# A two-layer float32 encoder on one core: the MLP's first product moved to seven block products, its hidden units taken in blocks of 3 and 4 pairs of chunks, sums into the residual stream by adding DMAs

## The chip, the cores and the metric

The kernel runs on one core of a Trainium2 chip. The metric is the device time of one execution in microseconds (us); the median of three runs is given below. The profile is of one more execution of the same program. Its engines are called PE (TensorE, with PEld for the loading of weights into it), DVE (VectorE), ACT (ScalarE), POOL (GpSimd) and SP (SyncE, which here only issues DMAs).

## What is computed

The input is x, 512 tokens of 1024 features in float32. Two layers follow, each made of a mixing part (differential attention and a recurrent branch side by side), a cross-attention over 256 memory tokens, and an MLP. The change concerns the end of each layer:

```
x = x + ox @ xa_wo                       # 1024 -> 1024, end of the cross-attention
hm = rms_norm(x, g_mlp)
x = x + square(relu(hm @ mlp_w1)) @ mlp_w2     # 1024 -> 4096 -> 1024
```

After the second layer comes a final RMS norm.

## The kernel before, in words

**Layout.** The residual stream lies feature-major in eight tiles `x[0]` to `x[7]` of 128 features by 512 tokens ("chunks"). A float32 product is made of three matmuls of rounded parts: each operand is split into a high part (ACT copies it with rounding) and a low part (DVE subtracts the high part), and PE adds high x high, high x low and low x high into one PSUM bank (`split`, line 429; `gemm_fm`, line 472).

**Two kinds of product.** `gemm_fm` makes one output chunk of 128 features by 512 tokens: 8 input chunks x 3 matmuls of 512 columns. Its weights need one load of 512 KB (`raw_weight`, line 439), one ACT copy and one DVE subtraction of 1024 elements per partition. `seven` (line 992) makes two output chunks at once as a 2 x 2 block product in seven block products instead of eight: inputs are taken in pairs of chunks, the tokens in two halves of 256 (`LO`, `HI`), and each of the seven products is (number of pairs) x 3 matmuls of 256 columns, 84 in all with four pairs. The sums of blocks that this needs are made on both sides: `right_pair` (line 957) makes for the weights three splits of 1024 elements, one of 512 and four sums of 512; `left_pair` (line 937) makes for one pair of input chunks three splits of 512 elements, one of 256 and four sums of 256, and leaves seven tiles. The results are seven half-tile DVE additions from PSUM into `x`.

**The stage around the change** (lines 1334 to 1360). Four `seven` add `ox @ xa_wo` to `x`; each chunk of `x` is then scaled and split by `prep_x` (line 559), which also adds its square to the norm's sum. Then the MLP's 4096 hidden units are taken in four blocks of eight chunks. `mlp_pair` (line 1185) makes two hidden chunks by two `gemm_fm` from the 16 tiles of split `x`, one DVE instruction each for ReLU and the norm's factor `rb`, one ACT square each, and then `left_pair`. For each block four `seven` add its part of the second product into `x`.

**Buffers.** Tag `b`, 62 tiles of 128 x 512 (line 37), holds nearly everything above: split `x`, hidden pairs and temporaries. Weights have 3 raw tiles, 3 high, 3 low and 4 tiles `pt` for sums; PSUM has 3 banks `mm` and 5 banks `at`.

**What sets the order.** The functions don't issue instructions; they record them with their dependences. `ISSUE` (lines 54 on) is a permutation, written out by hand for all recorded operations, and `Plan.order` and `Plan.emit` (lines 371 and 380) issue in that order. So every instruction of the kernel has line 391 in the profile, and its rows are told apart by tiles. Each engine works through its part of this order strictly; buffers come free as their last reader ends. Lines 522 to 525 issue eight small matmuls (`WARM`) on a constant tile at the start, whose result nobody reads. Ten weight tiles are loaded with POOL's queue, whose second load subtracts through a DMA that adds (`weight_dma`, line 449).

## Time and profile before

| what | value |
|---|---|
| median of 3 runs | 1442.62 us (1441.48 to 1444.51) |
| the profiled execution, its own time | 1441.38 us |
| its span in the profile | 1439.6 us |
| PE busy | 1419.9 us, 99% |
| PEld busy | 1238.2 us, 86% |
| DVE busy | 1157.9 us, 80% |
| ACT busy | 771.4 us, 54% |
| POOL busy | 44.1 us, 3% |
| mean DMA rate | 110 GB/s |

A row of grouped instructions reads: line, engine, operation, tile written <- tiles read, shape, count | busy us, mean ns of one | idle us of the engine before them and what ended it. A row of the timeline reads: start in us, length in us, engine, line, operation, tiles, shape, count, and in brackets the idle time before it with its releaser. A row of windows reads: stretch, its length, then busy us and (count) for PE, PEld, DVE, ACT and POOL, the granted share of PE's clock, the DMA engines' mean busy share and GB/s.

### The profile page before, as it was taken

How to read it: one execution, taken by the hardware profiler on the slowest of the kernel's cores; microseconds unless marked ns; L12 is line 12 of the kernel's file. 1: busy time of each engine (PE TensorE's matmuls, PEld its weight loads, DVE VectorE, ACT ScalarE, POOL GpSimd, SP SyncE). 2: the span in 40 equal slices, each digit the busy share in tenths (PEclk: the TensorE clock that was granted, in tenths of full speed). 3: DMA queues.
4: the chain of work that ended last, by engine and by line, in shares of the span. 5: the costliest groups of instructions: out<-in, count | busy, mean ns of one | idle time of the engine just before them, and what ended most of it. 6: DMA issues, size and time to landing. Idle time of an engine off the chain costs nothing.

```text
span 1439.6 us, 21603 instructions
## 1 busy us (share of the span) xinstructions
PE 1419.9 (99%) x8358; PEld 1238.2 (86%) x8358; DVE 1157.9 (80%) x2027; ACT 771.4 (54%) x1201; POOL 44.1 (3%) x69
## 2 busy tenths in 40 slices
PE   9999999999999999999999999999999999999997
PEld 7887887889989899898988879888898898989986
DVE  6899994669879596888868999755796886959797
ACT  5598864346454343435536987543554534435343
POOL 1000110000000000000000010000000000000001
PEclk9999999999999999999999999999999999999998
DMA  6455643211332323232334565432023223232322
GB/s 204 120 147 143 180 139 96 93 54 60 103 116 75 118 88 119 87 113 94 117 86 150 139 163 173 126 103 70 33 89 117 88 103 117 74 124 82 118 74 88
DMA packets 50262, 157.73 MB, mean 110 GB/s; under 512 B 6384, under 2 KB 8560, under 8 KB 50160
## 3 DMA queue, kind: packets, MB, share of 16 engines
q1 hardware_dynamic: 47136, 145.61, 30.8%
q0 software_dynamic: 2880, 10.49, 3.3%
q8 instruction: 66, 1.08, 0.3%
q14 instruction: 36, 0.29, 0.1%
q10 hardware_dynamic: 144, 0.26, 0.0%
HBM read 141.65 MB, written 2.10 MB: 100 GB/s over the span
## 4 chain that ended last, share of the span: by engine, by line
PE 81%; DVE 5%; DMA 1%; issue 1%; ACT 1%; POOL 0%; DVEq 0%; ACTq 0%; POOLq 0%
PE mm L391 61%; PE at L391 20%; DVE b L391 4%; DMA wlo<-in_W 1%; DVE s L391 1%; DVE wlo L391 1%; DVE pt L391 1%; ACT b L391 0%; DMA wraw<-in_W 0%; POOL s L391 0%; ACT whi L391 0%; ACT pt L391 0%; ACT wlo L391 0%; DVE c_x L391 0%; ACT rb L391 0%
## 5 line engine op out<-in xcount | busy, mean ns | idle before, releaser
L391 PE MATMUL mm<-b,whi 128*128 128x512 f32 (+1 forms) x3640 | 944.4, 348 | 1.3 <-ACT b L391 1.0
L391 PEld LDWEIGHTS mm<-b,whi 128*128 128x128 f32 x3640 | 622.1, 188 | 92.2 <-ACT b L391 1.4
L391 PE MATMUL mm<-b,wlo 128*128 128x512 f32 (+1 forms) x1820 | 629.6, 346 | 0.0
L391 PEld LDWEIGHTS mm<-b,wlo 128*128 128x128 f32 x1820 | 341.6, 188 | 47.8
L391 ACT ACTIVATE whi<-wraw 128x1024 fp32r<-128x1024 f32 (+1 forms) x205 | 213.6, 1044 | 234.1 <-PE mm L391 142.0
L391 DVE TENSOR_TENSOR wlo<-wraw,whi 128x1024 fp32r<-128x1024 f32 (+1 forms) x205 | 246.1, 1205 | 54.1 <-ACT whi L391 53.4
L391 DVE TENSOR_TENSOR b<-b,b 128x512 fp32r<-128x512 f32 (+3 forms) x420 | 241.2, 590 | 18.1 <-ACT b L391 14.3
L391 ACT ACTIVATE b<-b 128x512 fp32r<-128x512 f32 (+2 forms) x312 | 178.5, 596 | 123.4 <-DVE b L391 120.2
L391 ACT ACTIVATE whi<-pt 128x1024 fp32r<-128x1024 f32 x80 | 84.6, 1060 | 120.0 <-DVE pt L391 64.1
L391 PE MATMUL at<-b,whi 128*128 128x256 f32 x648 | 120.9, 279 | 0.0
L391 DVE TENSOR_TENSOR c_x<-c_x,mm 128x256 f32<-128x256 f32 (+1 forms) x176 | 76.2, 441 | 45.0 <-PE mm L391 44.2
L391 DVE TENSOR_TENSOR wlo<-pt,whi 128x1024 fp32r<-128x1024 f32 x80 | 97.5, 1220 | 6.0 <-ACT whi L391 5.1
L391 PEld LDWEIGHTS at<-b,whi 128*128 128x128 f32 x648 | 100.4, 189 | 2.1
L391 DVE SCALAR_TENSOR_TENSOR b<-mm,rb 128x512 f32<-128x512 f32 x80 | 54.8, 688 | 58.9 <-PE mm L391 53.2
L391 PE MATMUL at<-b,wlo 128*128 128x256 f32 x324 | 90.3, 279 | 0.0
L391 ACT ACTIVATE b<-at,s 128x512 f32<-128x512 f32 (+2 forms) x100 | 61.1, 616 | 38.1 <-DVE s L391 29.5
L391 PE MATMUL at<-b,pt 128*128 128x256 f32 x480 | 73.2, 279 | 0.0
L391 PEld LDWEIGHTS at<-b,pt 128*128 128x128 f32 x480 | 64.5, 188 | 1.6
L391 PE MATMUL at<-b,b 128*128 128x256 f32 (+1 forms) x320 | 64.2, 328 | 0.8 <-DVE pt L391 0.5
L391 DVE TENSOR_REDUCE s<-at 128x1 f32<-128x512 f32 (+1 forms) x80 | 54.1, 683 | 11.0 <-PE at L391 10.9
L391 PEld LDWEIGHTS at<-b,wlo 128*128 128x128 f32 x324 | 60.9, 188 | 0.0
L391 DVE TENSOR_TENSOR pt<-pt,wraw 128x512 f32<-128x512 f32 x80 | 54.9, 686 | 0.3
(129 smaller groups left out, 1275.6 us busy)
## 6 DMA issues: line engine op xcount, KB each, us to landing
wraw<-in_W SPq DMA_DIRECT2D x239, 512.0 KB, 3.3
b<-b SPq DMA_DIRECT2D x96, 128.0 KB, 3.9
whi<-in_W POOLq DMA_DIRECT2D x10, 512.0 KB, 4.7
wlo<-in_W POOLq DMA_DIRECT2D x10, 512.0 KB, 5.3
wraw<-in_memT SPq DMA_DIRECT2D x4, 512.0 KB, 4.4
out_T<-b SPq DMA_DIRECT2D x16, 128.0 KB, 1.8
c_x<-in_xT SPq DMA_DIRECT2D x7, 256.0 KB, 5.3
wraw<-in_W SPq DMA_DIRECT2D x6, 256.0 KB, 4.7
```

The source lines that it names most:

```text
L391: getattr(self.engines[op.eng], m)(*a, **k)
```

## The change

The first product of the MLP is made by the seven products too: `mlp_pair` takes the split `x` as four pairs (`left`, 4 x 7 tiles), uses `right_pair` on two weight tiles, and combines the seven results of 256 tokens into two hidden chunks. It returns them before `left_pair`, which is now made at the head of each block. The hidden units come in five blocks of 3, 3, 3, 3 and 4 pairs, so `right_pair` and `seven` work on widths of 768 for the first four, and `mlp_w2` is laid out to match. The additions into `x` become, for three of the four `seven` after the cross-attention and for all but the last `seven` of the MLP in each layer, an ACT copy of the PSUM half (negated where it is subtracted) and a DMA of POOL's queue that adds it to `x` in SBUF. The eight starting matmuls go. `ISSUE` is written anew as a whole (its string is not printed).

```diff
--- before.py
+++ after.py
@@ -32,8 +32,9 @@
 T_XO = 52
 T_W1 = 60
 T_W2 = 92
-T_G = 124
-NT = 126
+BLOCKS = (3, 3, 3, 3, 4)
+T_G = T_W2 + 8 * len(BLOCKS)
+NT = T_G + 2
 NRAW = 3
 NB = 62
 NW = 3
@@ -46,138 +47,167 @@
 LAG = 2
 POOL_OUT = (0, 1)
 DMA_T = (1, 4, 13, 36, 51)
-WARM = 8
+XO_FAR = (0, 2, 4)
+FAR = (4, 6)
 
...
@@ -436,14 +466,14 @@
 
     pre = {}
 
-    def raw_weight(l, t, ahead=None):
+    def raw_weight(l, t, ahead=None, w=1024):
         raw = plan.tile("wraw", [P, 1024], F32)
         if ahead:
             for h in range(2):
                 cs = slice(h * 512, h * 512 + 512)
                 SP.dma_start(out=raw[:, cs], in_=W[l * NT + t][:, cs])
         else:
-            SP.dma_start(out=raw, in_=W[l * NT + t])
+            SP.dma_start(out=raw[:, :w], in_=W[l * NT + t][:, :w])
         return raw
 
     def weight_dma(l, t):
@@ -517,12 +547,6 @@
     G.memset(ones, 1.0)
     mhalf = C([P, 4], F32, "mhalf")
     G.memset(mhalf, -0.5)
-
-
-    warm = AT()
-    with plan.group():
-        for _ in range(WARM):
-            PE.matmul(warm[:, :P], ones, ones, start=True, stop=True)
 
     class Norm:
 
@@ -954,59 +978,76 @@
                 5: (sh[:, LO], sl[:, LO]), 6: (sh[:, HI], sl[:, HI]),
                 7: (uh[:, LO], ul[:, LO]), 3: (uh[:, HI], ul[:, HI])}
 
-    def right_pair(l, ta, tb):
-
-        ra, rb_ = raw_weight(l, ta), raw_weight(l, tb)
-        b11, b21 = (ra.split_free(4, 2, P)[:, :, i, :] for i in range(2))
-        b12, b22 = (rb_.split_free(4, 2, P)[:, :, i, :] for i in range(2))
-
-        def hl():
-            return plan.tile("whi", [P, 1024], F32R), plan.tile("wlo", [P, 1024], F32R)
-
-        ah, al = hl()
-        split(ah, al, ra)
+    def right_pair(l, ta, tb, n=4):
+
+
+        w, m = n * 2 * P, n * P
+        ra, rb_ = raw_weight(l, ta, w=w), raw_weight(l, tb, w=w)
+        b11, b21 = (ra[:, :w].split_free(n, 2, P)[:, :, i, :] for i in range(2))
+        b12, b22 = (rb_[:, :w].split_free(n, 2, P)[:, :, i, :] for i in range(2))
+
+        def split_w(src):
+            hi, lo = plan.tile("whi", [P, 1024], F32R), plan.tile("wlo", [P, 1024], F32R)
+            split(hi[:, :w], lo[:, :w], src[:, :w])
+            return hi, lo
+
+        def halves(t):
+            v = t[:, :w].split_free(2, n, P)
+            return v[:, 0], v[:, 1]
+
+        ah, al = split_w(ra)
         t12 = plan.tile("pt", [P, 1024], F32)
-        t1, t2 = (t12.split_free(2, 4, P)[:, i] for i in range(2))
+        t1, t2 = halves(t12)
         V.tensor_tensor(t1, b11, b12, op=ALU.add)
         V.tensor_tensor(t2, t1, b22, op=ALU.add)
-        th, tl = hl()
-        split(th, tl, t12)
+        th, tl = split_w(t12)
         t34 = plan.tile("pt", [P, 1024], F32)
-        t3, t4 = (t34.split_free(2, 4, P)[:, i] for i in range(2))
+        t3, t4 = halves(t34)
         V.tensor_tensor(t3, b12, b22, op=ALU.add)
         V.tensor_tensor(t4, t2, b21, op=ALU.add)
         dh = plan.tile("pt", [P, 1024], F32R)
-        dv = dh.split_free(2, 4, P)
-        split(dv[:, 0], dv[:, 1], b22)
-        uh, ul = hl()
-        split(uh, ul, t34)
+        split(*halves(dh), b22)
+        uh, ul = split_w(t34)
 
         def at(hi, lo, o, st):
-            return [(hi[:, o + st * i:o + st * i + P], lo[:, o + st * i:o + st * i + P]) for i in range(4)]
-
-        out = {1: at(ah, al, 0, 256), 2: at(ah, al, 128, 256), 5: at(th, tl, 0, 128), 6: at(th, tl, 512, 128),
-               7: at(uh, ul, 0, 128), 4: at(uh, ul, 512, 128)}
-        out[3] = [(dh[:, i * P:(i + 1) * P], dh[:, 512 + i * P:512 + (i + 1) * P]) for i in range(4)]
+            return [(hi[:, o + st * i:o + st * i + P], lo[:, o + st * i:o + st * i + P]) for i in range(n)]
+
+        out = {1: at(ah, al, 0, 256), 2: at(ah, al, 128, 256), 5: at(th, tl, 0, 128), 6: at(th, tl, m, 128),
+               7: at(uh, ul, 0, 128), 4: at(uh, ul, m, 128)}
+        out[3] = [(dh[:, i * P:(i + 1) * P], dh[:, m + i * P:m + (i + 1) * P]) for i in range(n)]
         return out
 
-    def seven(l, ta, tb, left, ca, cb, order=range(4), early=False):
-
-
-        w = right_pair(l, ta, tb)
+    def product(w, left, i, bank, first):
+
+        for n, l_ in enumerate(left):
+            (wh, wl), (xh, xl) = w[i][n], l_[i]
+            o = bank[:, LO]
+            with plan.group():
+                PE.matmul(o, wh, xh, start=(first and n == 0), stop=False, skip_group_check=not first)
+                PE.matmul(o, wh, xl, start=False, stop=False, skip_group_check=not first)
+                PE.matmul(o, wl, xh, start=False, stop=(n + 1 == len(left)), skip_group_check=not first)
+
+    def seven(l, ta, tb, left, ca, cb, early=False, far=False):
+
+
+        w = right_pair(l, ta, tb, len(left))
         X, Y, Z = MM(), AT(), AT()
 
         def prod(i, bank, first):
-
-            for n, k in enumerate(order):
-                (wh, wl), (xh, xl) = w[i][k], left[k][i]
-                o = bank[:, LO]
-                with plan.group():
-                    PE.matmul(o, wh, xh, start=(first and n == 0), stop=False, skip_group_check=not first)
-                    PE.matmul(o, wh, xl, start=False, stop=False, skip_group_check=not first)
-                    PE.matmul(o, wl, xh, start=False, stop=(n == 3), skip_group_check=not first)
+            product(w, left, i, bank, first)
+
+        half = []
 
         def add(c, cs, bank, op):
-            V.tensor_tensor(x[c][:, cs], x[c][:, cs], bank[:, LO], op=op)
+            if not far:
+                V.tensor_tensor(x[c][:, cs], x[c][:, cs], bank[:, LO], op=op)
+                return
+            if not half:
+                t = T()
+                half.extend((t[:, LO], t[:, HI]))
+            t = half.pop(0)
+            A.activation(t, bank[:, LO], AF.Copy, scale=1.0 if op == ALU.add else -1.0)
+            G.dma_start(out=x[c][:, cs], in_=t, accum_op=ALU.add)
 
         prod(1, X, True)
         add(ca, LO, X, ALU.add)
@@ -1182,17 +1223,31 @@
             A.activation(te, out[0], AF.Copy)
             return left_pair(te, out[1])
 
-    def mlp_pair(l, bk, p, xs, rb):
-
-        ts = []
-        for i in (2 * p, 2 * p + 1):
-            pm = MM()
-            gemm_fm(l, T_W1 + 8 * bk + i, xs, pm)
-            t = T()
-            V.scalar_tensor_tensor(t, pm, 0.0, rb, op0=ALU.max, op1=ALU.mult)
-            A.activation(t, t, AF.Square)
-            ts.append(t)
-        return left_pair(*ts)
+    def mlp_pair(l, p, left, rb):
+
+        t = T_W1 + 2 * p
+        w = right_pair(l, t, t + 1)
+        X, Y, Z = MM(), AT(), AT()
+        ta, tb, u, v = T(), T(), T(), T()
+        product(w, left, 1, X, True)
+        A.activation(u[:, LO], X[:, LO], AF.Copy)
+        product(w, left, 2, Z, True)
+        V.tensor_tensor(ta[:, LO], u[:, LO], Z[:, LO], op=ALU.add)
+        product(w, left, 6, X, False)
+        A.activation(u[:, HI], X[:, LO], AF.Copy)
+        product(w, left, 5, Y, True)
+        A.activation(v[:, LO], Y[:, LO], AF.Copy)
+        product(w, left, 7, X, False)
+        V.tensor_tensor(tb[:, HI], v[:, LO], X[:, LO], op=ALU.subtract)
+        product(w, left, 3, Y, False)
+        V.tensor_tensor(tb[:, LO], Y[:, LO], u[:, HI], op=ALU.subtract)
+        product(w, left, 4, X, False)
+        V.scalar_tensor_tensor(ta[:, HI], X[:, LO], 0.0, rb[:, HI], op0=ALU.max, op1=ALU.mult)
+        V.scalar_tensor_tensor(ta[:, LO], ta[:, LO], 0.0, rb[:, LO], op0=ALU.max, op1=ALU.mult)
+        V.scalar_tensor_tensor(tb, tb, 0.0, rb, op0=ALU.max, op1=ALU.mult)
+        for x_ in (ta, tb):
+            A.activation(x_, x_, AF.Square)
+        return ta, tb
 
 
     def drain(gen):
@@ -1333,21 +1388,35 @@
             ox.append(hd.pv())
         nrm = Norm()
         xs = [None] * KD
+        left = []
         for m in range(0, 8, 2):
-            seven(l, T_XO + m, T_XO + m + 1, ox, m, m + 1)
-            for c in (m, m + 1):
-                xs[c] = prep_x(l, "g_mlp", c, nrm)
+            seven(l, T_XO + m, T_XO + m + 1, ox, m, m + 1, far=m in XO_FAR)
+            te, to = T(), T()
+            for c, t in ((m, te), (m + 1, to)):
+                A.activation(t, x[c], AF.Copy, scale=pc(l, "g_mlp", c))
+                nrm.add(x[c])
+            left.append(left_pair(te, to))
         rt, rb = finish_norm(nrm)
-        hid = [mlp_pair(l, 0, p, xs, rb) for p in range(4)]
-        for bk in range(4):
-            nxt = [mlp_pair(l, bk + 1, 0, xs, rb)] if bk < 3 else []
-            if bk == 3:
+        xs = [None] * KD
+        pairs = iter(range(sum(BLOCKS)))
+
+        def hidden():
+            return mlp_pair(l, next(pairs), left, rb)
+
+        first = hidden()
+        for bk, n in enumerate(BLOCKS):
+            hid = [left_pair(*first)] + [left_pair(*hidden()) for _ in range(n - 1)]
+            last = bk + 1 == len(BLOCKS)
+            end = last and l + 1 == DEPTH
+            if last:
                 nrm = Norm()
                 xs = [None] * KD
+            else:
+                first = hidden()
             for m in range(0, 8, 2):
-                end = l + 1 == DEPTH and bk == 3
-                seven(l, T_W2 + 8 * bk + m, T_W2 + 8 * bk + m + 1, hid, m, m + 1, early=end and m == 6)
-                for c in (m, m + 1) if bk == 3 else ():
+                t = T_W2 + 8 * bk + m
+                seven(l, t, t + 1, hid, m, m + 1, early=end and m == 6, far=(bk, m) < FAR)
+                for c in (m, m + 1) if last else ():
                     if not end:
                         xs[c] = prep_x(l + 1, "g_mix", c, nrm)
                     elif m < 6:
@@ -1355,9 +1424,6 @@
                     if end and c in POOL_OUT:
                         xs[c] = T()
                         A.activation(xs[c], x[c], AF.Copy, scale=gfin(c))
-            if bk < 3:
-                nxt += [mlp_pair(l, bk + 1, p, xs, rb) for p in range(1, 4)]
-            hid = nxt
 
@@ -1408,10 +1474,13 @@
...
-        w2 = f["mlp_w2"][l].reshape(4, 1024, 1024)
+        w2, at = f["mlp_w2"][l], 0
...
-        tiles += [_fm(w2[j]) for j in range(4)]
+        for n in BLOCKS:
+            t = _fm(w2[at:at + 2 * n * P])
+            tiles.append(np.concatenate([t, np.zeros((8, P, 1024 - 2 * n * P), np.float32)], 2))
+            at += 2 * n * P
...
```

## Rows read from the trace of the kernel before

**Rows 1.** The page: span, and part 1, busy us of each engine.
```profile
span 1439.6 us, 21603 instructions
...
PE 1419.9 (99%) x8358; PEld 1238.2 (86%) x8358; DVE 1157.9 (80%) x2027; ACT 771.4 (54%) x1201; POOL 44.1 (3%) x69
```

**Rows 2.** Windows: output product and MLP of each layer.
```profile
341.00:716.00 375.00, 374.94 (x2424) 338.12 (x2425) 306.90 (x512) 173.51 (x239) 1.86 (x1) 1.00 0.29 100
1051.00:1427.00 376.00, 375.72 (x2458) 339.47 (x2456) 306.23 (x517) 170.95 (x235) 1.71 (x2) 1.00 0.27 94
```

**Rows 3.** Timeline of PE, matmuls of 512 columns.
```profile
500.01 0.63 PE L391 MATMUL mm<-b,whi 128*128 128x512 f32 x2
...
500.71 0.63 PE L391 MATMUL mm<-b,whi 128*128 128x512 f32 x2
```

**Rows 4.** Timeline of PE, matmuls of 256 columns.
```profile
516.45 0.39 PE L391 MATMUL at<-b,whi 128*128 128x256 f32 x2
516.68 0.28 PE L391 MATMUL at<-b,wlo 128*128 128x256 f32 x1
516.79 0.39 PE L391 MATMUL mm<-b,whi 128*128 128x256 f32 x2
```

**Rows 5.** Timeline of DVE in a stretch without waits.
```profile
509.99 0.69 DVE L391 TENSOR_TENSOR b<-b,b 128x512 fp32r<-128x512 f32 x1
510.59 0.41 DVE L391 TENSOR_TENSOR c_x<-c_x,at 128x256 f32<-128x256 f32 x1
510.92 0.42 DVE L391 TENSOR_TENSOR b<-b,b 128x256 fp32r<-128x256 f32 x1
511.26 1.22 DVE L391 TENSOR_TENSOR wlo<-wraw,whi 128x1024 fp32r<-128x1024 f32 x1
512.39 0.42 DVE L391 TENSOR_TENSOR b<-b 128x256 f32<-128x256 f32 x1
```

**Rows 6.** Groups by form, whole span: DVE additions into x; ACT copies.
```profile
L391 DVE TENSOR_TENSOR c_x<-c_x,mm 128x256 f32<-128x256 f32 x160 | 65.4, 417 | 30.8 <-PE mm L391 29.9
...
L391 DVE TENSOR_TENSOR c_x<-c_x,at 128x256 f32<-128x256 f32 x121 | 49.1, 415 | 2.6 <-PE at L391 2.5
...
L391 ACT ACTIVATE b<-b 128x256 fp32r<-128x256 f32 x40 | 16.3, 409 | 0.5
```

**Rows 7.** Windows: stretches of seven products, of 512-column products, and of attention.
```profile
342.00:382.00 40.00, 40.00 (x328) 39.24 (x327) 38.93 (x68) 23.04 (x32) 0.00 (x0) 1.00 0.27 93
438.00:485.00 47.00, 47.00 (x350) 44.44 (x349) 35.15 (x60) 18.63 (x23) 0.00 (x0) 1.00 0.25 91
563.00:612.00 49.00, 49.00 (x250) 41.18 (x249) 35.79 (x59) 22.30 (x34) 0.00 (x0) 1.00 0.29 102
100.00:180.00 80.00, 77.36 (x449) 65.98 (x448) 79.09 (x144) 67.07 (x116) 8.06 (x9) 1.00 0.60 164
```

**Rows 8.** Part 6 of the page: two DMA issues, KB each, us to landing.
```profile
b<-b SPq DMA_DIRECT2D x96, 128.0 KB, 3.9
...
wlo<-in_W POOLq DMA_DIRECT2D x10, 512.0 KB, 5.3
```

**Rows 9.** Timeline of POOL: an adding DMA is issued.
```profile
88.98 0.88 POOL L391 DMA_DIRECT2D wlo<-in_W  x1 [5.37 <-ACT wlo L391]
```

**Rows 10.** Timeline of DVE beside that issue.
```profile
88.18 1.89 DVE L391 TENSOR_TENSOR b<-b,b 128x512 f32<-128x512 f32 x3
```

**Rows 11.** Timeline of PE at the start.
```profile
2.09 3.78 PE L391 MATMUL at<-c_ones 128*128 128x128 f32 x16 [2.09 <-POOL c_mhalf L391]
5.66 0.42 PE L391 MATMUL at<-s,c_ones 128*128 128x2 f32 x2
...
9.61 0.63 PE L391 MATMUL at<-whi,b 128*128 128x512 f32 x1
10.04 0.63 PE L391 MATMUL at<-wlo,b 128*128 128x512 f32 x1
...
11.25 0.62 PE L391 MATMUL at<-whi,b 128*128 128x512 f32 x2
```

280 lines of the change are left out of this document (154 added, 126 removed).

## The prediction, made before the changed kernel was run

> **What bounds the kernel now.** I began with the page: PE is busy for 1419.9 of 1439.6 us, DVE for 1157.9 [rows 1]. Matmuls overlap, so that alone does not prove PE full; the spacing of their starts does. Three matmuls of 512 columns start within 0.70 us, 0.233 each [rows 3], three of 256 within 0.34 us, 0.113 each [rows 4], and in the two stages that the change rewrites (the output product of the cross-attention, and the MLP) the groups follow each other like this: 768 x 0.233 + 1680 x 0.113 = 179 + 190 = 369 us of matmuls per layer in stages of 375 and 376 us [rows 2]. The stage is PE's, with 1.8% lost.
>
> Next I asked how far DVE is from being the bound. Its instructions also overlap by some 0.09 us, so I count from start to start: 0.60 us for 512 elements, 0.33 for 256, 1.13 for 1024 [rows 5]. DVE is busy for 307 and 306 us of these stages [rows 2], unevenly: 38.9 of 40 us while the seven products of the cross-attention run, 35.8 of 49 where the 512-column products run [rows 7]. The change puts its DVE work where the slack is now.
>
> **The change, part by part, for one layer.**
>
> *PE.* The first product had 32 chunks x 24 = 768 matmuls of 512 columns; it gets 16 pairs x 84 = 1344 of 256. That is 179 against 152 us, 27 less. The second product keeps its 1344 (sixteen `seven` of 63, four of 84). PE then has 3024 x 0.113 = 342 us in the stage, 348 with the same 1.8%.
>
> *DVE, first product.* One pair now costs two subtractions of 1024, two instructions of 512 and `left_pair`. Afterwards: `right_pair`, 3 x 1.13 + 5 x 0.60 = 6.39 us; five instructions of 256 and one of 512 that combine the products, 2.28; `left_pair`, 3 x 0.60 + 5 x 0.335 = 3.48. That is 12.1 us against 6.9, over 16 pairs 194 against 111. PE needs 9.5 us for such a pair: **here DVE is the slower engine**.
>
> *DVE, second product.* For three pairs, by estimates between the steps of rows 5 (0.87 us for 768 elements, 0.47 for 384), `right_pair` costs 4.93 us; sixteen of these and four of 6.39 make 104. Of the additions into `x` one `seven` in the layer stays, 2.3 us. Before, it was 16 x (6.39 + 7 x 0.33) = 139; now 107.
>
> *DVE, output product.* Four `right_pair` (25.6), seven additions (2.3), the norm's seven sums (4.2), four `left_pair` in place of `prep_x` (13.9): 46, against 44.
>
> *The adding DMAs.* Today there are 281 half-tile additions into `x` on DVE [rows 6], seven for each of 40 `seven` and one more in the last; eight more `seven` make it 337. 22 of 24 `seven` in a layer lose theirs: 154 per layer, 308 in all, and 29 stay. Each becomes an ACT copy, at most 0.41 us [rows 6], 63 us per layer on an engine that is busy for 173 of 375 [rows 2]; the other new ACT work (16 pairs, one split of 1024 and one of 512 more each, and three copies) adds some 45 us. ACT reaches about 280 of 360 and stays off the path. POOL gets 154 issues of 0.88 us [rows 9], 136 us, on a queue that is idle there. DMA engines are at 0.27 to 0.29 in these stages [rows 2]; 154 x 128 KB is 20 MB more per layer against some 37 MB, so they stay below one half.
>
> *The sum.* DVE: 194 + 107 + 46, plus the split of the next layer's input (eight times two instructions, 9.6 us; the last layer only squares, 3): 356.5 and 350 us. The first `right_pair` can be made in the stage before, where DVE has slack, as today: 350 and 343.5. So DVE at 350 and 343.5 and PE at 342 to 348 are both full. DVE has held 97% beside a full PE (342 to 382 us) and 99% where PE lost 3% (100 to 180 us) [rows 7]; I take 98%, which gives 357 and 350.5. On top come the block boundaries. First-product pairs (DVE 12.1, PE 9.5) and `seven` of three pairs (DVE 4.9, PE 7.1) balance only if they are mixed, but of 62 tiles `b` the split `x` holds 28 and a block of hidden units 21; 13 are left for the next block, the results under way to DMAs and temporaries. If nothing could be mixed beyond the one pair that is written ahead, a layer's MLP would take 9.5 + 4 x (27.8 + 38) + 39.9 + 38 = 350.6 us against 301 of DVE work, 9.9 us per block. Thirteen tiles hold two pairs that `left_pair` has not yet widened (4 tiles) with their temporaries, so most can be mixed: I take 1.5 us per block from between 0 and 9.9, 7.5 per layer. The start of the MLP waits for one more link (scale, then `left_pair`) and for the DMA's landing: 1 us per layer, from 0 to 10 (third rival).
>
> 365.7 and 359 against 375 and 376: 26 us less.
>
> *The start.* Without the eight matmuls PE's first work is at 5.66 us in place of 2.09 [rows 11]. The 512-column matmuls at 9.61 and 10.04 us are 0.43 apart, the lower of PE's two clock levels (1.2 GHz), and one is 0.63 us long; at 11.25 two together take 0.62 [rows 11], the upper level (2.4 GHz). If the rise comes later by the whole 3.6 us, matmuls of 3.6 us take twice their time: 1.8 us lost; if not, none. I take 1.
>
> From the profiled execution, 1441.4 - 25 = 1416.4; the median of before stands 1.2 higher, so **1417 us**, its own range 1400 to 1434 (DVE's 98% taken as 100% or 96%, boundaries 0 or 4 us).
>
> **A rule that would change a term.** The adding DMA's landing is the term with no row of its own: 3.9 us for a 128 KB copy on SP's queue, 5.3 us for 512 KB added on POOL's [rows 8]; I take 3.9 to 5.3, and the upper in the rival below. In the Trainium skill, "DMA: Bandwidth & Descriptors", section "Anatomy of one DMA", such a DMA takes about 2.0 us and its bytes at 436 GB/s; that makes 2.3 us, an estimate from that page, and by it the third rival would vanish (9 us of POOL per `seven`, under PE's 9.5). No row here shows so short a landing on that queue.
>
> **The rivals.**
>
> 1. *PE stays the bound.* Mixing is perfect and DVE runs at 100% or hands work to its neighbours (the next layer's first product needs only the first chunks). Stages of 348 and 348: 55 us less, 1389 us. For it: DVE's slack just before and after the stage. Against: DVE's own 350.
>
> 2. *First product and second product run in turns* (the slower side). The 62 tiles don't let the pairs of the next block be made while a block is in use; PE waits for DVE in each row of pairs, and DVE idles beside the `seven`. Then 350.6 + 39.6 for the output product = 390 against 375.5, 29 more, and 1 for the start: 1473 us. It is slower from the point where the boundaries cost over some 5 us per block. For it: before, too, the two kinds form separate stretches, 438 to 485 and 563 to 612 [rows 7]. Against: a finished pair needs only two tiles until it is widened.
>
> 3. *POOL's queue is late.* Three of the seven additions go to a half that an earlier one is still adding to, so the queue must wait for that landing: issues at 0, 5.3, 6.2, 7.1, 12.4, 13.3 and 14.2 us, 15 us per `seven`, while PE makes one of four pairs in 9.5. Behind the waiting issue stand all later additions, and POOL's small powers for the norms. After the output product the third pair of `x` would be whole some 13 us after PE's last matmul; 3 to 8 us of first-product matmuls on other pairs cover a part. The same holds for the last block, at the end too. 5 to 10 us at four places: about 1447 us, 1425 to 1460. For it: 15 against 9.5. Against: additions of different halves and `seven` can be put between.
>
> 4. *POOL's issues stop DVE.* If DVE stood while POOL makes an adding DMA, 308 x 0.88 = 271 us would come on top of a full DVE, about 1690 us. The row beside such an issue speaks against it: three subtractions in a row took 1.89 us (0.60, 0.60 and the last one's 0.69) over the issue at 88.98 [rows 9, 10]. The Trainium skill, "SBUF — State Buffer", section "SBUF: two separate sides", says that DVE with two SBUF inputs and a POOL operation that reads SBUF exclude each other for the whole instruction. By that rule such an issue would have to show in DVE's row if it reads SBUF; it doesn't.
>
> **How the numbers follow.** Forecast 0.44, rival 1 0.20, rival 2 0.20, rival 3 0.12, rival 4 0.04. What a measurement here can tell from no change is about 0.2%, 2.9 us. The forecast and rival 1 are faster (0.64); of rival 3 a third falls below, of rival 2, whose boundary cost can stop anywhere between 5 and 9.9 us or just short of 5, 0.03; 0.02 and 0.04 of the two lie within the bound. Faster 0.71, same 0.06, slower 0.23. The range 1390 to 1458 leaves out rival 4, the upper half of rival 2 and the lower edge of rival 1.
>
> **What would show it.** Right: no 512-column matmul in the MLP, 3024 matmuls of 256 columns per stage; DVE at 95% or more from the output product to the end of the MLP; stages near 366 and 359 us; 308 POOL issues, 29 or so half-tile additions left on DVE. PE's idle time, if any, before first-product matmuls, ended by DVE's `wlo`. Rival 1: DVE below 95% with PE at 99%. Rival 2: stretches with PE at 80% and DVE full, next to stretches with DVE at 75%. Rival 3: ACT's scaling of `x`, or the last block's norm, waits for a DMA into `c_x`. Rival 4: DVE instructions longer than 0.69 us for 512 elements. The forecast is wrong if DVE's steps change length beside 308 DMAs, or if PE waits at the boundaries for more than 4 us each.

## The result, and the profile after

The changed kernel takes **1462.11 us** (median of four runs, 1456.28 to 1467.5), the kernel before beside it 1443.57 (1441.48 to 1444.51): a ratio of **1.0137, interval 1.0111 to 1.0163**. It is 1.4% slower, where 1417 us was forecast and 1458 was the upper end of the range. The profiled execution took 1466.83 us with a span of 1465.0, against 1441.38 and 1439.6 of before. Of the four runs two took 1456 and 1457 us at a mean granted clock of 0.990 and 0.991 and two, the profiled one among them, 1467 us at 0.985, so the profile shows some 5 us more than the median.

First, where the 25.4 us of span lie. Three landmarks of a layer can be read in both timelines: the last exponential of the cross-attention (ACT), the first small power of the norm after the MLP (POOL), and the last exponential of the next layer.

| stretch (us) | before | after | forecast | measured |
|---|---|---|---|---|
| start to the last exponential, layer 0 | 336.4 | 339.8 | +1 | +3.4 |
| output product and MLP, layer 0 | 401.5 | 421.8 | -9.3 | **+20.3** |
| mixing and attention, layer 1 | 307.7 | 307.8 | 0 | +0.1 |
| output product and MLP, layer 1 | 380.1 | 383.0 | -17 | **+2.9** |
| the rest | 13.9 | 12.6 | 0 | -1.3 |

(These stretches hold some work of their neighbours too: the two of before stand for stages of 375 and 376 us in [rows 2], so 26.5 and 4.1 us are no part of the stage.) Both stages missed the forecast, the first by 30 us, the second by 20.

The page of the kernel after, its span, its engines, the chain of waits by engine, the sums' issues and the sums' landing, and last, from the view of tile `c_x`, the spread of that landing, against [rows 1, 8]:

```profile
span 1465.0 us, 25303 instructions
...
PE 1396.9 (95%) x9494; PEld 1273.8 (87%) x9494; DVE 1257.4 (86%) x2207; ACT 959.6 (65%) x1732; POOL 318.7 (22%) x377
...
PE 58%; DVE 13%; issue 11%; DMA 9%; ACT 7%; POOL 3%; SPq 0%; DVEq 0%; ACTq 0%; POOLq 0%
...
L421 POOL DMA_DIRECT2D c_x<-b x308 | 274.1, 1491 | 568.1 <-ACT b L421 520.8
...
c_x<-b POOLq DMA_DIRECT2D x308, 128.0 KB, 5.4
...
DMA to landing us min/median/max: 2.6/5.4/9.0
```

The work is what was forecast: 308 sums by DMA, POOL busy with them for 274 us (0.89 each), DVE 100 us up. But PE is no longer busy for 99% of the span, and the DMAs stand in the chain with 9%. The sums land after 5.4 us in the median, just above the upper end of what I had taken (5.3), and one by one after 2.6 to 9.0 us: the 38 that are issued with no other sum under way take 3.0 us in the median, the other 270 take 5.7. By the estimate of 2.3 us from the Trainium skill, "DMA: Bandwidth & Descriptors", section "Anatomy of one DMA", they would land in less than half of the median; the shortest of this trace come near it, the bursts do not.

Windows of the kernel after (stretch, its length, busy us and count of PE, PEld, DVE, ACT and POOL, granted share of PE's clock, DMA share, GB/s), first the stage of layer 0, then of layer 1, against [rows 2]:

```profile
341.00:375.00 34.00, 31.25 (x252) 29.66 (x252) 31.14 (x50) 25.39 (x47) 11.42 (x13) 1.00 0.59 128
375.00:418.00 43.00, 40.31 (x312) 38.93 (x312) 40.67 (x72) 29.72 (x51) 7.08 (x9) 0.92 0.39 103
418.00:445.00 27.00, 22.22 (x167) 21.18 (x166) 23.20 (x46) 15.47 (x28) 3.66 (x1) 0.91 0.16 53
445.00:500.00 55.00, 49.52 (x403) 49.02 (x403) 47.16 (x82) 36.28 (x72) 23.39 (x27) 0.92 0.72 160
...
620.00:680.00 60.00, 54.83 (x451) 54.47 (x450) 52.90 (x90) 38.63 (x77) 13.39 (x15) 0.94 0.54 139
680.00:740.00 60.00, 57.88 (x477) 55.95 (x476) 52.89 (x86) 40.77 (x73) 31.55 (x38) 1.00 0.78 163
...
1075.00:1150.00 75.00, 68.28 (x560) 65.50 (x559) 69.63 (x116) 53.82 (x94) 19.22 (x22) 1.00 0.51 120
1150.00:1180.00 30.00, 25.20 (x201) 23.75 (x202) 29.94 (x60) 20.99 (x40) 4.78 (x6) 1.00 0.28 78
...
1300.00:1360.00 60.00, 59.52 (x506) 58.77 (x505) 57.43 (x99) 42.36 (x81) 24.98 (x28) 1.00 0.71 163
```

Four things are to be seen. In the head of a stage (output product and first block, 341 to 445 and 1075 to 1180) PE is idle for 10 to 12 us beside a DVE that is busy for 91% and 95%. In layer 0 PE loses time later too, with DVE below 90% (445 to 500, 620 to 680). The granted clock is below 1 in four of these stretches; before, it was 1.00 in both stages [rows 2]. And in layer 0, behind the head, the DMA engines are busy for 0.54 to 0.78 of the time; the prediction had them below one half.

What stops PE there shows in the waits (engine, who waited for whom: us in total, times, longest):

```profile
POOL c_x L421 <- DMA c_x<-b: 31.9, 15, 4.0
ACT b L421 <- DMA c_x<-b: 28.9, 17, 5.4
...
PE mm L421 <- ACT b L421: 21.6, 17, 5.2
...
DVE b L421 <- DMA c_x<-b: 9.5, 3, 5.4
```

and in the timeline of one such place, DVE, ACT, PE and POOL in turn, and last two pieces of the chain of waits there (start, length, what):

```profile
473.66 1.23 DVE L421 TENSOR_TENSOR wlo<-wraw,whi 128x1024 fp32r<-128x1024 f32 x1 [0.16 <-ACT whi L421]
480.27 0.69 DVE L421 TENSOR_TENSOR b<-b,b 128x512 fp32r<-128x512 f32 x1 [5.38 <-DMA c_x<-b]
...
475.50 0.41 ACT L421 ACTIVATE b<-b 128x256 fp32r<-128x256 f32 x1
482.13 0.63 ACT L421 ACTIVATE pt<-wraw 128x512 fp32r<-128x512 f32 x1 [6.23 <-DVE wlo L421]
...
477.81 0.28 PE L421 MATMUL mm<-b,wlo 128*128 128x256 f32 x1
483.09 0.80 PE L421 MATMUL mm<-b,whi 128*128 128x256 f32 x2 [5.01 <-ACT b L421]
483.68 0.41 PE L421 MATMUL mm<-b,wlo 128*128 128x256 f32 x1
483.90 0.63 PE L421 MATMUL mm<-b,whi 128*128 128x256 f32 x2
...
473.63 5.37 POOL L421 DMA_DIRECT2D c_x<-b  x6 [0.90 <-DMA c_x<-b]
481.12 8.06 POOL L421 DMA_DIRECT2D c_x<-b  x9 [2.13 <-DMA c_x<-b]
...
473.63 0.54 POOL c_x L421
474.16 6.02 DMA c_x<-b
```

DVE is ready at 474.89 for an ordinary subtraction and must not write: its tile `b` was last a staging tile, the copied halves of a sum, and the DMA that reads it has not landed. That DMA stands in POOL's queue, which itself waited for a landing (0.90 us) and then issues six sums one after the other; the one that DVE needs is the second of them, issued at 474.16 and landed 6.02 us later. So DVE stands for 5.38 us, ACT behind it for 6.23, PE behind both for 5.01. When PE starts again, its matmuls at 483.68 and 483.90 are 0.22 us apart in place of 0.113 [rows 4]: the lower of its two clock levels (1.2 GHz), which holds for 6.8 us here.

In this trace the clock is at its lower level for 34 us before the end, in seven places, each beside a pause of PE (0.98 to 5.17 us); the two longest pauses have the two longest falls in the stages. A pause of 2.56 us at 597.8 had none. Before, the clock fell nowhere ahead of the end.

### The profile page after: what moved, and what is told of

The parts are those of the page before. It is cut to its first block, busy times and chain, and to the rows that moved or that the text cites. A ratio compares the mean times of both kernels' runs of the same rounds, so it can differ in the third digit from the quotient of the medians.

```text
span 1465.0 us, 25303 instructions
## 1 busy us (share of the span) xinstructions
PE 1396.9 (95%) x9494; PEld 1273.8 (87%) x9494; DVE 1257.4 (86%) x2207; ACT 959.6 (65%) x1732; POOL 318.7 (22%) x377
## 4 chain that ended last, share of the span: by engine, by line
PE 58%; DVE 13%; issue 11%; DMA 9%; ACT 7%; POOL 3%; SPq 0%; DVEq 0%; ACTq 0%; POOLq 0%
PE mm L421 39%; PE at L421 19%; DVE b L421 6%; DMA c_x<-b 6%; ACT b L421 4%; DVE wlo L421 3%; DVE pt L421 3%; POOL c_x L421 2%; DMA wraw<-in_W 2%; ACT whi L421 1%; ACT L421 1%; DMA b<-b 0%; POOL s L421 0%; DMA wlo<-in_W 0%; ACT pt L421 0%
## 5 line engine op out<-in xcount | busy, mean ns | idle before, releaser
L421 PE MATMUL mm<-b,whi 128*128 128x256 f32 (+1 forms) x3640 | 823.5, 318 | 28.7 <-ACT b L421 21.6
L421 PE MATMUL mm<-b,wlo 128*128 128x256 f32 (+1 forms) x1820 | 574.9, 316 | 6.1 <-DVE wlo L421 5.8
L421 POOL DMA_DIRECT2D c_x<-b x308 | 274.1, 1491 | 568.1 <-ACT b L421 520.8
L421 DVE TENSOR_TENSOR wlo<-wraw,whi 128x1024 fp32r<-128x1024 f32 (+2 forms) x181 | 208.8, 1155 | 41.6 <-ACT whi L421 41.2
L421 ACT ACTIVATE whi<-wraw 128x1024 fp32r<-128x1024 f32 (+2 forms) x181 | 180.8, 1003 | 81.9 <-PE mm L421 41.1
L421 PE MATMUL at<-b,whi 128*128 128x256 f32 x1160 | 220.9, 282 | 4.1 <-DVE b L421 2.9
L421 ACT ACTIVATE whi<-pt 128x1024 fp32r<-128x1024 f32 (+1 forms) x160 | 155.8, 975 | 53.5 <-DVE pt L421 36.3
L421 DVE TENSOR_TENSOR wlo<-pt,whi 128x1024 fp32r<-128x1024 f32 (+1 forms) x160 | 178.3, 1114 | 10.4 <-ACT whi L421 9.5
L421 ACT ACTIVATE b<-mm 128x256 f32<-128x256 f32 x240 | 88.7, 379 | 81.9 <-PE mm L421 63.7
L421 DVE TENSOR_TENSOR pt<-pt,wraw 128x512 f32<-128x512 f32 (+1 forms) x160 | 101.4, 634 | 1.1
```

Of the source, the lines that this page charges most:

```text
L421: getattr(self.engines[op.eng], m)(*a, **k)
```

## The experiments

Two theories were put to the runs. **D**: DVE is the bound, full along the stage, and the first product's extra work on it is what the time went to. **H**: the adding DMAs take the time, as their landings hold the staging tiles (part B below) and the readers of `x`, and the pauses bring the clock down. The kernel of before stands at 1442 to 1444 us beside each run.

**1. The adding DMAs left out** (`no_sums`: they are recorded and not issued; the ACT copies stay, so these 308 sums are missing in `x`).

```diff
             G.dma_start(out=x[c][:, cs], in_=t, accum_op=ALU.add)
+            plan.ops[-1].skip = True
```

> The changed kernel with its 308 adding DMAs left out (the ACT copies of the PSUM halves stay, the order of all else stays; x lacks these sums). Theory H (the adding DMAs hold things up: a landing takes 5.4 us, ACT waited 28.9 us for staging tiles that a DMA still read, the two longest idle stretches of PE, 5.0 and 5.2 us, follow such waits, and PE's clock fell to its lower level next to them): those two stretches and most of the clock's falls go, 20 to 25 us less, about 1440 us. Theory D (DVE is the bound wherever first-product pairs stand alone, above all from the output product to the first seven of the MLP): at most 8 us less, about 1455.

Measured: 1431.46 us (ratio 0.9929, 0.9907 to 0.9951), 31 us less than the changed kernel, more than H had expected (20 to 25). H carries: the sums' DMAs cost 31 us, and without them the change is a gain of 0.7%. Windows of this run, head and rest of each layer's stage:

```profile
341.00:445.00 104.00, 95.00 (x765) 89.98 (x764) 100.43 (x178) 74.45 (x134) 3.81 (x3) 1.00 0.22 76
445.00:740.00 295.00, 293.47 (x2400) 287.02 (x2399) 272.76 (x460) 203.58 (x386) 3.04 (x4) 1.00 0.34 112
1075.00:1180.00 105.00, 97.21 (x800) 94.81 (x799) 103.10 (x183) 74.26 (x137) 1.39 (x1) 0.98 0.29 95
1180.00:1420.00 240.00, 237.35 (x2003) 235.61 (x2001) 226.78 (x388) 168.78 (x326) 2.93 (x5) 0.99 0.29 97
```

Here the two parts of a stage are plain: in the head DVE is full (100.4 of 104 us, 103.1 of 105) and PE is idle for 8 to 9 us, after it PE is busy for 293.5 of 295 and 237.4 of 240 us and DVE has 5 to 8% to spare. Busy time makes PE's loss too small, as a matmul that stands alone is busy for 0.28 us and in a row takes 0.113 [rows 4]; by the starts of the matmuls, wherever two are over 0.122 us apart, the heads lose 13 and 15 us and the rest of the stages 4 and 3.

**2. All sums back on DVE** (`near`): the DVE addition from PSUM at the place of each ACT copy.

```diff
...
-            A.activation(t, bank[:, LO], AF.Copy, scale=1.0 if op == ALU.add else -1.0)
-            G.dma_start(out=x[c][:, cs], in_=t, accum_op=ALU.add)
+            V.tensor_tensor(x[c][:, cs], x[c][:, cs], bank[:, LO], op=op)
...
```

> The changed kernel with the sums into x made by DVE again, each at the place of its ACT copy; no adding DMAs, no staging tiles. DVE gets 308 x 0.33 = 102 us more, 51 per layer. Theory H: the waits for landings go (about 20 us) and the added DVE work is partly hidden: 1450 to 1480 us. Theory D: DVE, full already, passes nearly all of it on: 1530 us or more.

Measured: 1571.78 us (1.0891, 1.0851 to 1.093), 110 more than the changed kernel for 102 us of DVE (308 x 0.33). In this order DVE has no room for them; by its waits PE stood 47.9 us for DVE's additions to leave a bank `mm`, against 2.1 in the changed kernel. So the DMAs are a way out of something dearer, in an order that was made for them.

**3. Half of the weights' low parts left out** (`light`): the subtraction makes 512 of 1024 elements, and the products read these twice; DVE has some 58 us less per layer.

```diff
-            split(hi[:, :w], lo[:, :w], src[:, :w])
+            A.activation(hi[:, :w], src[:, :w], AF.Copy)
+            V.tensor_tensor(lo[:, :m], src[:, :m], b(hi[:, :m]), op=ALU.subtract)
...
```

> The changed kernel with half of each low part of the weights left out in the seven products (three subtractions of 1024 elements become 512 each, or of 768 become 384; PE reads the first half twice), all else and the order the same. DVE has some 58 us less per layer, PE the same. Theory D: PE becomes the bound of the start of the MLP and between blocks, 40 us less or more, at most 1420 us. Theory H: the landings still hold ACT, at most 15 us less, about 1450 us.

Measured: 1443.27 us (1.0006, 0.999 to 1.0022), 19 less. That lies between: DVE costs time, but 116 us of it less by the count of its instructions (103 by the pages' busy times) give back only 19, and ACT still waits 32.7 us for sums to land.

**4. The adding DMAs alone, in the kernel before** (`before_far`, 252 of them; its first product stays, and what `more` holds is issued in place of the addition).

```diff
             V.tensor_tensor(x[c][:, cs], x[c][:, cs], bank[:, LO], op=op)
...
+            o = plan.ops[-1]
...
+            o.more = [("act", "activation", (t, bank[:, LO], AF.Copy), {"scale": 1.0 if op == ALU.add else -1.0}),
+                      ("pool", "dma_start", (), {"out": x[c][:, cs], "in_": t, "accum_op": ALU.add})]
```

> The kernel before with the adding DMAs alone: for all seven products but the last of each stage, the DVE addition into x is replaced at its place by an ACT copy and an adding DMA (252 of them). DVE has 83 us less, PE the same. Theory H: staging tiles and landings stop ACT here too, 10 us slower or more, 1453 us or above. Theory D: PE stays the bound and DVE has more room: between 1436 and 1446 us.

Measured: 1505.72 us (1.0435, 1.0416 to 1.0454), 63 more than before, though DVE's busy time fell from 80% to 72%. A row of its waits, and its windows at the end of the output product and of the last block in layer 0:

```profile
ACT b L391 <- DMA c_x<-b: 55.5, 16, 8.0
```

```profile
341.00:400.00 59.00, 47.88 (x341) 44.98 (x342) 35.70 (x53) 30.66 (x55) 18.12 (x21) 0.88 0.53 118
724.00:760.00 36.00, 25.97 (x147) 23.71 (x148) 15.47 (x22) 14.90 (x26) 6.95 (x8) 0.81 0.40 93
```

All of these ACT instructions read `x`: here the sums cost by their readers, up to 8.0 us at a time, and no ACT or DVE wait for a landing is for a staging tile. What the added ACT copies cost beside the DMAs was not tried apart. This is rival 3 of the prediction at the places that it named; this order was not made for it.

**5. Both reliefs** (`both`: 1 and 3 together; the sums and half of the low parts are missing).

> The changed kernel with both: the 308 adding DMAs left out and half of the weights' low parts left out (58 us less of DVE per layer). If DVE's load and the adding DMAs are all that keeps the change from its PE time, this reaches it: 1385 to 1400 us, PE at 98% in the rewritten stages. If the new order itself loses time elsewhere (ACT's copies that free PSUM, waits of the order), it stays at 1415 us or more.

Measured: 1419.61 us (0.9842, 0.9816 to 0.9868). So something is left beyond DVE and the DMAs. The trace shows what: 256-column matmuls in a row start either 0.1133 or 0.1179 us apart (experiment 12), and here 66% and 53% of those of the two stages are of the wider kind, 3024 x 0.0046 x (0.66 + 0.53) = some 17 us over both layers; the rest lies mainly in the heads, which lose 20 us by the starts of the matmuls, in pauses of at most 1.7 us.

**6. PE relieved** (`pe_light`): high x low left out in the MLP's first product (`two` is true there alone), some 101 us of PE in all.

```diff
                 PE.matmul(o, wh, xh, start=(first and n == 0), stop=False, skip_group_check=not first)
-                PE.matmul(o, wh, xl, start=False, stop=False, skip_group_check=not first)
+                if not two:
+                    PE.matmul(o, wh, xl, start=False, stop=False, skip_group_check=not first)
                 PE.matmul(o, wl, xh, start=False, stop=(n + 1 == len(left)), skip_group_check=not first)
```

> The changed kernel with one of the three matmuls of each triple (high x low) left out in the MLP's first product: 896 matmuls of 256 columns less in the two layers, 101 us of PE at 0.113. Theory D (DVE is the bound wherever first-product pairs run): nearly nothing comes of it, at most 15 us less, 1447 us or more. If PE were still the bound of these stretches: 60 us less or more.

Measured: 1444.31 us (1.0016, 0.9999 to 1.0034), 18 less for 101 us of PE. PE is not what sets the time of the first product; like 3, no relief of one engine alone is worth much.

**7. The soon-read sums back on DVE** (`ends_near`): the output product's and those of each layer's last block, 84 in all, 28 us of DVE; the other 224 stay DMAs.

```diff
+            if far == "soon":
+                V.tensor_tensor(x[c][:, cs], x[c][:, cs], bank[:, LO], op=op)
...
+                return
...
-            seven(l, T_XO + m, T_XO + m + 1, ox, m, m + 1, far=m in XO_FAR)
+            seven(l, T_XO + m, T_XO + m + 1, ox, m, m + 1, far=m in XO_FAR and "soon")
```

> The changed kernel with the sums of the output product and of the MLP's last block, which are read soon after, made by DVE at the places of the ACT copies (84 of 308; 28 us more of DVE in all); the other 224 stay adding DMAs. Part R of theory H (readers of x wait for landings: ACT 12.7 us, and POOL's own waits): these waits go and outweigh the DVE work, 1450 to 1462 us. Theory D: DVE passes its 28 us on, 1480 us or more.

Measured: 1498.46 us (1.0407, 1.0366 to 1.0449), 36 more than the changed kernel. The landings that readers of `x` wait for (12.7 us of the waits above, by tiles) cost less than DVE at these places.

**8. Staging tiles of their own** (`own`): the copied halves of 38 of the 176 staging tiles lie in buffers that are idle at that time (tags `Cr`, `Sr`, `xb`), not in `b`. The order of all instructions stays.

```diff
+    for r in sorted(plan.stages, key=lambda r: min(use[r])):
+        for tag, n in (("Cr", 1), ("Sr", 1), ("xb", 2)):
...
+                r.tag = tag
```

> The changed kernel with 38 of its 176 staging tiles moved from the 62 shared tiles to the buffers of the rotary tables and of the convolution, which stand idle in these stages; the order of all instructions is the same. Part B of theory H (the shared tiles are held until a DMA has landed, and ACT or DVE waits for one: 25.7 us of such waits): some of those waits go, 4 to 10 us less, 1452 to 1458 us. If holding tiles does not matter: within 3 us of the changed kernel.

Measured: 1451.27 us (1.0063, 1.0045 to 1.0081), 11 less. Its waits for landings, against those of the changed kernel above:

```profile
POOL c_x L422 <- DMA c_x<-b: 29.3, 16, 4.9
ACT b L422 <- DMA c_x<-b: 13.2, 12, 2.6
DVE b L422 <- DMA c_x<-b: 4.8, 1, 4.8
```

POOL waits nearly as long, ACT 15.7 us less and never over 2.6. That the holding of shared tiles costs time is shown: a fifth of the staging moved gives back 11 us (some 4 either way by the two intervals), about a third of the 31. It is the better form of the change, still 0.6% slower than before.

**9. The sums by POOL itself** (`pool_add`, the first two lines), and **10. a sum of weights on POOL as well** (`pool_t3`, all four).

```diff
-            G.dma_start(out=x[c][:, cs], in_=t, accum_op=ALU.add)
+            G.tensor_tensor(x[c][:, cs], x[c][:, cs], t, op=ALU.add)
...
-        V.tensor_tensor(t3, b12, b22, op=ALU.add)
+        G.tensor_tensor(t3, b12, b22, op=ALU.add)
```

> After the change, but the 308 sums are made by POOL itself: one POOL addition (x and the copied half, both in SBUF) at the place where the DMA was issued. The DMA's issue (0.89 us of POOL, 274 us in all), its landing (5.4 us) and the staging tile held for that long go; a POOL instruction comes, by the four POOL instructions of 256 elements at the end of the kernel 0.73 us each, some 225 us in all, with no landing behind it. Theory H (the adding DMAs cost time because their landings hold staging tiles and the readers of x, and PE's clock falls in the pauses): nearly all of what leaving them out gave comes back, 1430 to 1442 us, no wait of ACT ended by a sum longer than 2 us, and DVE's instructions as long as before. Rival E (a POOL addition stops a DVE instruction with two inputs in SBUF, and nearly all of DVE's here have two, so a full DVE loses up to 308 x 0.73 = 225 us): 1550 to 1690 us, and DVE rows longer than 0.69 us for 512 elements. Rival N (where the sums are made doesn't matter, the ACT copies and the order do): 1455 to 1465 us.

> The kernel with the sums on POOL, and one of the four sums of weight blocks in each of the 80 weight pairs of 16 or 12 blocks moved from DVE to POOL as well (512 or 384 elements per partition, 0.60 or 0.47 us of DVE each, some 45 us of DVE in all; 1.0 to 1.5 us of POOL each by an estimate from its 0.73 us for 256 elements, some 100 us of a POOL that then has 320). If DVE bounds the stage and POOL doesn't disturb it: 12 to 25 us less than the kernel with the sums on POOL (halving the low parts took 116 us of DVE for 19 us). If POOL's work stops DVE: no less, or more. If POOL is late with the weight sum, since it stands behind additions that wait for PE: more, with PE waiting for DVE's sums and splits of weights.

Measured: 1560.92 us (1.0809, 1.0791 to 1.0827), and 1586.81 (1.0988, 1.097 to 1.1007). Rival E carries. Groups by form of DVE with the sums on POOL, ahead of them the same groups of the changed kernel (busy us, mean ns):

```profile
L421 DVE TENSOR_TENSOR wlo<-pt,whi 128x1024 fp32r<-128x1024 f32 x96 | 117.1, 1220 | 8.1 <-ACT whi L421 7.8
L421 DVE TENSOR_TENSOR pt<-pt,wraw 128x512 f32<-128x512 f32 x96 | 65.9, 686 | 0.6
...
L421 DVE TENSOR_TENSOR b<-b,mm 128x256 f32<-128x256 f32 x32 | 13.3, 417 | 2.8 <-PE mm L421 2.8
```

```profile
L421 DVE TENSOR_TENSOR wlo<-pt,whi 128x1024 fp32r<-128x1024 f32 x96 | 133.5, 1391 | 6.5 <-ACT whi L421 6.4
...
L421 DVE TENSOR_TENSOR pt<-pt,wraw 128x512 f32<-128x512 f32 x96 | 87.0, 906 | 0.6
...
L421 DVE TENSOR_TENSOR b<-b,mm 128x256 f32<-128x256 f32 x32 | 13.2, 414 | 0.1
```

With two inputs in SBUF the mean grows, 0.686 to 0.906 us for 512 elements; with one of them in PSUM it doesn't. DVE's busy time grows from 1257.4 to 1383.8 us (in `pool_t3`, with 80 DVE instructions fewer, to 1401.6), and POOL's additions take 1.36 us each where such an instruction took 0.73 at the end of the kernel. The Trainium skill, "SBUF — State Buffer", section "SBUF: two separate sides", says that a DVE instruction with two SBUF inputs and a POOL operation that reads SBUF hold each other off for the whole instruction; these rows agree. Whether POOL's lateness adds to the time of these two kernels was not tried apart. The rows also settle rival 4 of the prediction: an addition on POOL does that, the issue of an adding DMA doesn't. The same group has 686 ns in the changed kernel, beside 308 issues, and 686 ns in the kernel before.

**11. The starting matmuls put back** (`warm`), and **12. the kernel before once more** (`before_again`), one execution each.

> After the change with the eight starting matmuls put back, one look. It is also a second look at the stages of the changed kernel. If the removal of the starting matmuls cost something, PE's clock rises and the first norm's factor comes up to 1.8 us earlier than in the run after the change (rise at 9.96 us, factor at 30.7 us); by the forecast's term 1 us; if they do nothing here, both lie within 0.5 us. If the falls of PE's clock belong to the order of the instructions, they come at the same places (near 375, 395, 423, 443, 481 and 665 us); if they follow pauses that only some executions have, some of the places differ, and the time moves with them by 1.7 us for each 3.4 us at the lower level, between 1450 and 1468 us.

> The kernel before, unchanged, for a second trace. In the traces so far 256-column matmuls in a row start either 0.113 or 0.118 us apart, for hundreds at a time, and PE's time can't be had from one of them alone. If the spacing belongs to the place in the program (tiles, banks), the wide one comes in the same stretches (350 to 370, 440, 610 to 640, 680 to 710 us); if it is set anew after each break, it lies elsewhere in this execution, with a share anywhere from a quarter to three quarters.

The first took 1469.38 us. PE's clock rises near 10 us with them as without, and the norm's first factor comes at 31.2 us against 30.7: in this execution the starting matmuls were worth nothing. PE pauses at the same places of layer 0 as in the run after the change (422, 483, 598 and 670 us; 2.40, 4.39, 2.56 and 6.24 us), so the pauses belong to the order; of the falls of the clock some moved (none at 375, 396 and 444; one at 167, one at 597 and one at 1123).

The second took 1441.34 us. Timeline of PE at the same place of layer 1, the earlier trace of before first, then this one:

```profile
1078.90 0.28 PE L391 MATMUL at<-b,wlo 128*128 128x256 f32 x1
1079.01 0.39 PE L391 MATMUL mm<-b,whi 128*128 128x256 f32 x2
1079.24 0.28 PE L391 MATMUL mm<-b,wlo 128*128 128x256 f32 x1
```

```profile
1078.62 0.28 PE L391 MATMUL at<-b,wlo 128*128 128x256 f32 x1
1078.74 0.40 PE L391 MATMUL mm<-b,whi 128*128 128x256 f32 x2
1078.97 0.28 PE L391 MATMUL mm<-b,wlo 128*128 128x256 f32 x1
```

Three starts take 0.34 us in the one and 0.35 in the other, and so on for hundreds of matmuls on either side (the means over all are 0.1133 and 0.1179). Most stretches keep their kind from one execution to the next (610 to 640, 680 to 710, 1150 to 1170 us are wide in both), some don't (350 to 360, 1070 to 1085). Neither half of what was expected holds alone.

**13 and 14. Where DVE costs time** (`head_light`, `body_light`): without the DMAs as in 1, and the low parts halved as in 3, but only in the first 8 weight pairs of each layer's stage, or only in the other 32.

```diff
+        light = plan.hl[0] < 8
+        plan.hl[0] += 1
...
-            split(hi[:, :w], lo[:, :w], src[:, :w])
+            if light:
+                A.activation(hi[:, :w], src[:, :w], AF.Copy)
+                V.tensor_tensor(lo[:, :m], src[:, :m], b(hi[:, :m]), op=ALU.subtract)
+            else:
+                split(hi[:, :w], lo[:, :w], src[:, :w])
```

> Without the adding DMAs (their sums into x are left out), and with half of the low parts of the weights left out in the first 8 weight pairs of each layer's stage alone: the four of the output product and the first four of the hidden units. DVE loses 8 x 1.6 = some 13 us per layer there, a fifth of what the kernel with both reliefs lost (58). If DVE binds only in the head of the stage: nearly the whole difference between that kernel (1419.6 us) and the one without the DMAs (1431.5 us) comes from here, 1417 to 1424 us. If DVE binds evenly: a fifth of it, 1428 to 1431 us.

> The same, but the low parts are halved in the other 32 weight pairs of each layer's stage alone (some 45 us of DVE per layer). If DVE binds only in the head: no gain, 1429 to 1434 us, with PE at 99% from the first matmul of the second product on and what DVE doesn't need left idle. If DVE binds evenly: four fifths of the difference, 1420 to 1424 us.

Measured: 1424.33 us (0.9868, 0.9849 to 0.9887) and 1424.01 (0.9862, 0.9844 to 0.988), each 7 us below the kernel without the DMAs. Windows of the first and then of the second, of layer 0 and the head of layer 1:

```profile
341.00:445.00 104.00, 99.26 (x796) 94.81 (x795) 94.81 (x189) 77.96 (x144) 1.47 (x3) 0.98 0.22 76
445.00:740.00 295.00, 293.57 (x2402) 286.94 (x2401) 273.01 (x461) 203.42 (x386) 3.04 (x4) 1.00 0.34 112
1075.00:1180.00 105.00, 99.06 (x838) 96.94 (x837) 100.17 (x190) 77.86 (x145) 1.39 (x1) 1.00 0.28 95
```

```profile
341.00:445.00 104.00, 96.56 (x764) 91.52 (x763) 98.66 (x180) 74.40 (x135) 3.81 (x3) 0.98 0.22 76
445.00:740.00 295.00, 294.05 (x2411) 288.58 (x2410) 238.19 (x466) 205.01 (x389) 3.04 (x4) 1.00 0.34 112
1075.00:1180.00 105.00, 97.78 (x809) 95.58 (x809) 97.26 (x186) 74.89 (x139) 1.39 (x1) 0.98 0.29 99
```

The head carries the larger weight: 26 us less of DVE there give 7, 0.27 us for each, against 90 us elsewhere for the same 7, 0.08 for each (by count; the pages' busy times fall by 23 and 79). In the windows of the first the head's PE moves: it makes 796 and 838 matmuls in the heads in place of 765 and 800, 69 more, which at 0.113 to 0.118 us are 8 us. In those of the second it makes 764 and 809; after the head PE was nearly full already. But the body's 7 us were not expected by the head alone, the intervals are some 3 us wide on either side, and the profiled execution of the second is its slowest (1428.68 us), so its gain is hardly in its windows. The wide spacing differs too (43% and 73% of the two stages without the DMAs, 39% and 33% in the first, 57% and 61% in the second; 6 us less for the first). That DVE binds in the head is shown; that it costs nothing behind it is not.

## Why the prediction was wrong

**The adding DMAs were mis-sized, and this turned the sign.** The forecast gave them 1 us per layer, at the start of the MLP, and called their issues "a queue that is idle". They cost 31 us (1); without them the kernel takes 1431 us and is a gain, still 14 us above the forecast. Rival 3 had the mechanism in part (its 1425 to 1460 us came near the 1462 with half of the cause): POOL's queue waits for a landing before it may add to the same half again (31.9 us in 15 waits, 0.9 and 2.13 us in the rows at 473.63 and 481.12), then issues in bursts. It priced the readers of `x` alone. What it didn't see is the other end of the DMA: the copied half lies in a tile `b` of the 62 that everything shares, and stays taken until the DMA has been issued and has landed. The wait then falls on the instruction of DVE or ACT that is next to write this tile, and on all behind it in order (25.7 of the 38.4 us for which ACT and DVE waited for these landings are of this kind by their tiles, 12.7 are readers of `x`). The kernel's order of operations, matched with the trace one by one, splits the 25.7: 14.1 us fall on ACT copies of later sums, 11.6 on work that has nothing to do with the sums, as the 5.38 us above. By the same matching a copied half waits 8 us in the median until its DMA is issued and 14 until it has landed (78 at most), and up to 14 staging tiles are held at once, where the prediction had 13 tiles for these, the next block and all temporaries. Run 8 shows the cost of it by a third. The prediction's sentence that ACT "stays off the path" at 280 of 360 us failed for the same reason: its mean says nothing of the 5 us in which it stands. So did the sentence that the DMA engines stay below one half (0.54 to 0.78 from 445 us on in layer 0, against 0.34 in run 1 without the sums).

**The clock was not in the sum.** A pause of PE was priced at its own length. Beside the pauses PE ran for 34 us at 1.2 GHz in the profiled run, up to 17 us of work lost (what of it lay within the pauses cost nothing). Without the sums' DMAs it was 7 us of such clock (1), with a fifth of the staging moved 14 (8), so of what these runs gave back a part is clock; how much is not shown. In layer 0, which lost 20.3 us, stand six of the seven falls and pauses of 5.01, 5.17, 2.56 and 2.37 us; layer 1, with no pause over 1.9 us and no fall, lost 2.9.

**DVE at 98% of the whole stage was the wrong sum.** The forecast compared totals, 350 us of DVE against 342 of PE, and put the places that can't be mixed at 1.5 us per block boundary. By its own steps the head alone tells more: the output product and the four pairs made ahead of the second product are 46 + 4 x 12.1 = 94 us of DVE against 8 x 9.5 = 76 of PE, and no matmul of the second product exists yet to fill the 18 us (run 1 showed 13 and 15 lost there). Behind it PE is the bound, 342 - 76 = 266 us. That makes 360 us, and 6 and 10 us of wide spacing (43% and 73% of 3024 matmuls) 366 and 370: without the DMAs the stages were 367.1 and 371.7 (393.6 - 26.5, 375.8 - 4.1). The forecast's 365.7 for layer 0 came out near by another way, its 359 for layer 1 was 13 us low: 7 us of that is a smaller total of DVE, which saves nothing in the head. This sum was made after the runs, and 2 us of agreement are not a test of it. Runs 13 and 14 bear the head out by its larger weight, not as the only place. Between blocks PE was full without the DMAs, so the 1.5 us per boundary was too much, if anything, and rival 2 (turns) did not come. The forecast's own range, 1400 to 1434, was also narrower than its two bounds: taken together, 98% as 100 or 96% and 0 or 4 us per boundary make about 1388 to 1457.

**PE's own term held, its pitch did not quite.** 27 us less per layer from 1344 matmuls in place of 768 is right at equal spacing, and 9494 against 8358 matmuls on the page are as counted. The 0.113 us came from one stretch [rows 4]; the 1.8% that was added for losses is about the wide spacing, which in `both` took 9 and 7 us, where 6 was allowed.

**The start** was taken at 1 us; run 11, one execution, shows none. What came in its place is 2.76 us of pause at 123 us in the attention of layer 0, with a fall of the clock beside it, in the runs after the change; this part of the +3.4 us was not looked into.

**Right**: DVE's instructions kept their length beside 308 DMAs (against rival 4), and rival 1 (PE alone, 1389) did not come; even with DVE and DMAs relieved the kernel came to 1420. Of the marks that were named, "PE waits at the boundaries for more than 4 us each" showed, in two places, as waits for landings, and DVE stood at 89% and 95% behind the heads, not above 95 all along.

What stays open: the split of the 31 us between staging, readers, POOL's queue and clock beyond the third that run 8 gave back, and why layer 0 has the long pauses and layer 1 doesn't; only a new order of all instructions would try it. Of the kernels here that leave no work out, none beats the kernel before.

## What to carry to other kernels

When a sum, a copy or a store goes to a DMA, count what its source buffer is worth from the copy to the landing, queue included: in a kernel with shared buffers and a fixed order the bill comes at whatever writes that buffer next, which can be an instruction that has nothing to do with it. Compare two engines' totals only over stretches in which their work can be mixed; a head in which one of them has all the surplus is added, not averaged. And on an engine kept at its upper clock, a pause can cost more than its length.

## What was not expected of the hardware

- A row of 256-column matmuls with a weight load each has two steady spacings, 0.1133 and 0.1179 us, held for up to hundreds of matmuls; of the switches between runs of at least four, 48 of 51 come at a break in the row in the kernel before and 42 of 47 in `both`, and the share of the wide kind was 22 to 73% from stage to stage. That is up to 10 us per layer here.
- PE's granted clock fell beside pauses as short as 0.98 to 1.78 us (at 375, 395 and 442 us) and did not beside one of 2.56 us (at 598 us), which had a fall of 6.8 us in another execution (`warm`).
- An addition on POOL and a DVE instruction with two SBUF inputs go with longer times of both (0.686 to 0.906 us, 0.73 to 1.36); 308 issues of adding DMAs by the same engine leave DVE's 0.686 as it was.
- The adding DMAs of POOL's queue landed after 2.6 us at the shortest, 5.4 in the median and 9.0 at the longest for the same 128 KB; the median was 3.0 for those issued with no other sum under way and 5.7 for the others.
